# The state-space stage's output products one gate unit later, with one more buffer of four of its tiles

## The chip, the core and the metric

The kernel runs on one core of one Trainium2 chip. The metric is device microseconds of one execution; lower is better. Times of the trace are microseconds from the start of the profiled execution's span.

## What is computed

One layer of a flow-matching backbone on 128 context tokens and 1024 latent tokens, width 1024. The normed input `h` is multiplied by `w_in`, whose columns feed three things: the input of a bidirectional state-space branch (512 columns, 32 groups of 16), the input of a Fourier branch (512 columns), and two sigmoid gates of 1024 columns each. Cut to what matters here:

```
z = h @ p["w_in"]
u_s5, u_f, g_s5, g_f = ...        # 512, 512, 1024, 1024 columns
bu = einsum("nlgh,gph->nlgp", u, bb)              # into 64 complex states for each group
s = associative_scan(a, bu) + cumulated_a * h0    # along the tokens, in both directions
y = einsum("nlgp,ghp->nlgh", s_re, c_re) - einsum("nlgp,ghp->nlgh", s_im, c_im)
y = y + s5_d * u                                  # summed over both directions
m = sigmoid(g_s5) * (y_s5 @ w_proj_s5) + sigmoid(g_f) * (y_f @ w_proj_fft)
```

The layer goes on with `w_out`, a gated MLP and a last norm.

## The kernel before

Tokens are put in chunks of T = 8: 144 chunks (CC), of which 16 are context. The 32 groups are done in NB = 8 blocks of GQ = 4 groups, both directions side by side on the 128 partitions. A block q passes through three functions:

- `prep(q)` (`s5_prep` and `s5_prep2`) makes on DVE the tables W and G (lines 545 to 561), transposes G on PE (`gtr`, line 566), forms the in-chunk kernel on PE (`kx`, line 594) and DVE (KX, line 597), and sends KX by DRAM into the Toeplitz table T (lines 601 to 605). It begins by loading Bp and Cp, and by clearing `bb` (line 576), which the `kx` products of the block before must have read.
- `s5_run(q)` loads U, multiplies it on PE with G (the four PSUM tiles `v{q}_00`, `_02`, `_10`, `_12`, line 621), copies these into the states X on ACT (lines 625, 629) and DVE (lines 627, 630), and scans X in place on DVE: 14 steps of four dependent instructions (lines 636 to 639).
- `s5_out(q)` copies X, shifted, into Xo on ACT (lines 656 to 658) and multiplies on PE: T with U (line 666) and W with Xo (lines 667, 668), into the two PSUM tiles `y{q}_0`, `y{q}_2`.

The PSUM tiles `gtr`, `kx`, `v` and `y` take turns in three buffers (tag `aux`). So `v{q}_12` can begin only when DVE's copy of `v{q}_00` (line 630) has freed a buffer.

Between these calls stand nine gate units `gate(p)` of the order ORD = (0, 1, 2, 3, 4, 5, 8, 6, 7). Each has two halves f, and each half is 72 matmuls of 128x384 (lines 271 to 273; `g60_2` is the unit 6, half 0, token tile 2), in three precision-split products: the weights are split into a high part on ACT (line 93) and a low part on DVE (line 94, `wh_g600` and `wh_g601` for the two 512-column pieces of `g60`). The gates need nothing of the scans; they are PE work that can stand between the state-space steps. The unit after the loop is `uf20` (the second half of the Fourier input).

The order on each engine is not that of the code. A scheduler reorders the calls' instructions at build time, engine by engine, by its own estimates; each engine then runs its list strictly in that order, and waits at an instruction whose operands or buffers are not ready. SP's list holds the loads in the same way.

Of the kernel before, what the change touches and what calls it, by code (L numbers as in the profile page):

```python
# [10 lines left out]
F32 = mybir.dt.float32  # L11
# [18 lines left out]
T = 8  # L30
CP, CS = NP // T, NS // T
CC = CP + CS
GQ = 4
GU = 8
NB = G // GQ
# [2 lines left out]
NBG = 10  # L38
NUF = 3
NSG = 4  # L40
NW = 3
ORD = (0, 1, 2, 3, 4, 5, 8, 6, 7)
EPS = 1e-6
TW = 2 * 7 * 4 * 64
# [17 lines left out]
def tile_flow_step(ctx: ExitStack, tc: tile.TileContext, a, o):  # L62
# [459 lines left out]
    q5 = open_pool("q5", side="right")  # L522

    def s5_prep(q):
# [16 lines left out]

        W = q5.tile([128, 2, GQ * 128], F32, tag="W", bufs=NW, name=f"W{q}")
        Gt = q5.tile([128, 2, GQ * 128], F32, tag="G", bufs=NG, name=f"G{q}")
# [27 lines left out]
    def s5_prep2(q, gs, Bp, Cp, W, Win):  # L571
        bb = q5.tile([128, 3, 2, GQ * H + H], F32, tag="bb", name=f"bb{q}")
        b4 = bb[:, :, :, 0:GQ * H].rearrange("p v r (g h) -> p v r g h", g=GQ)
        bt1 = q5.tile([128, 240], F32, tag="KX", name=f"bt1{q}")[:, 0:2 * GQ * H].rearrange("p (r g h) -> p r g h", r=2, g=GQ)
        shb = [128, GQ, H]
        V.memset(bb, 0.0)
        for ri in range(2):
            fb = [fr2[:, r, gs].unsqueeze(2).to_broadcast(shb) for r in range(2)]
            V.tensor_tensor(b4[:, 0, ri], Bp[:, ri], fb[0], ALU.mult)
            V.tensor_tensor(bt1[:, ri], Bp[:, 1 - ri], fb[1], ALU.mult)  # L580
            V.tensor_tensor(b4[:, 0, ri], b4[:, 0, ri], bt1[:, ri],
                            ALU.subtract if ri == 0 else ALU.add)
        V.tensor_copy(bb[0:64, 1], bb[0:64, 0])
        V.tensor_copy(bb[64:128, 2], bb[64:128, 0])
        KX = q5.tile([128, GQ // 4, 240], F32, tag="KX", name=f"KX{q}")
        for aa in range(GQ // 4):
            ps = aux_tile(f"kx{q}_{aa}")
            for v, cs_ in ((2, slice(0, 112)), (0, slice(112, 128)), (1, slice(128, 240))):
                for ri in range(2):
                    for g4 in range(4):  # L590
                        g = 4 * aa + g4
                        src = (Cp[:, ri, g], W[:, ri, 128 * g:128 * g + 112],
                               W[:, ri, 128 * g + 16:128 * g + 128])[v]
                        PE.matmul(ps[32 * g4:32 * g4 + 32, cs_], bb[:, v, ri, H * g:H * g + 32], src,
                                  start=(ri == 0), stop=(ri == 1), skip_group_check=True)
            S.copy(out=KX[:, aa], in_=ps[:, 0:240])
            V.scalar_tensor_tensor(KX[:, aa, 112:128], eyeq, dq[:, GQ // 4 * q + aa:GQ // 4 * q + aa + 1],
                                   ps[:, 112:128], ALU.mult, ALU.add)
        kd = Kd[q]
        for g4 in range(4):  # L600
            SY.dma_start(out=kd[:, g4::4, :], in_=KX[32 * g4:32 * g4 + 16])
        Tm = q5.tile([128, GQ, 128], F32, tag="T", bufs=2, name=f"T{q}")
        win = bass.AP(tensor=kd.tensor, offset=kd.offset,
                      ap=[[16, T], [GQ * 240, H], [240, GQ], [1, 128]])
        SY.dma_start(out=Tm, in_=win)
        return W, Win, Tm

    def s5_run(q, Win):
        gs = slice(GQ * q, GQ * q + GQ)
        U = q5.tile([128, GQ, CC], F32, tag="U", bufs=2, name=f"U{q}")  # L610
        u0 = GQ * q % GU
        SY.dma_start(out=U, in_=Ud[GQ * q // GU].rearrange("s h (g c) -> (s h) g c", g=GU)[:, u0:u0 + GQ, :])
        X = q5.tile([128, 2, GQ, CC + 1], F32, tag="X", bufs=2, name=f"X{q}")
        V.memset(X[:, :, :, 0:1], 0.0)
        n = 0
        for ri in range(2):
            for g0 in range(0, GQ, 2):
                ng = 2
                ps = aux_tile(f"v{q}_{ri}{g0}")
                for g in range(ng):  # L620
                    PE.matmul(ps[:, CC * g:CC * g + CC], Win[:, ri, 128 * (g0 + g):128 * (g0 + g) + 128],
                              U[:, g0 + g, :], start=True, stop=True)
                v = ps[:, 0:CC * ng].rearrange("p (g c) -> p g c", g=ng)
                xg = X[:, ri, g0:g0 + ng]
                S.copy(out=xg[0:64, :, 1:CC + 1], in_=v[0:64])
                if n % 2:
                    V.tensor_copy(xg[64:128, :, CP + 1:CC + 1], v[64:128, :, CC - 1:CP - 1:-1])
                else:
                    S.copy(out=xg[64:128, :, CP + 1:CC + 1], in_=v[64:128, :, CC - 1:CP - 1:-1])
                V.tensor_copy(xg[64:128, :, 1:CP + 1], v[64:128, :, CP - 1::-1])  # L630
                n += 1
        def step(lv, dst, src):
            m = dst.shape[3]
            shp = [128, 2, GQ, m]
            A, B = (q5.tile([128, 2, GQ, CC // 2], F32, tag=f"{z}{q % 2}", name=f"{z}{q}_{lv}_{m}")[:, :, :, 0:m] for z in ("ta", "tb"))
            V.tensor_tensor(A, src, Sc[:, 0, lv, gs].unsqueeze(1).unsqueeze(3).to_broadcast(shp), ALU.mult)  # L636
            V.tensor_tensor(B, src, Sg[:, :, lv, gs].unsqueeze(3).to_broadcast(shp), ALU.mult)
            V.tensor_tensor(dst, dst, A, ALU.add)
            V.tensor_tensor(dst, dst, B[:, ::-1], ALU.add)  # L639

        for lv in range(4):
            d = 1 << lv
            step(lv, X[:, :, :, 2 * d:CC + 1:2 * d], X[:, :, :, d:CC + 1 - d:2 * d])
        V.tensor_copy(fin[:, :, gs], X[:, :, :, CP])
        V.tensor_copy(X[:, :, :, CP], h0[:, :, gs])
        for lv in range(4, 7):
            d = 16 << (lv - 4)
            step(lv, X[:, :, :, CP + d:CC:16], X[:, :, :, CP:CC - d:16])
        for lv in (3, 2, 1, 0):
            d = 1 << lv  # L650
            step(lv, X[:, :, :, 3 * d:CC + 1:2 * d], X[:, :, :, 2 * d:CC + 1 - d:2 * d])
        return U, X

    def s5_out(q, W, Tm, U, X):
        Xo = q5.tile([128, 2, GQ, CC], F32, tag="Xo", name=f"Xo{q}")
        S.copy(out=Xo[0:64], in_=X[0:64, :, :, 0:CC])
        S.copy(out=Xo[64:128, :, :, 0:CP], in_=X[64:128, :, :, CP - 1::-1])
        S.copy(out=Xo[64:128, :, :, CP:CC], in_=X[64:128, :, :, CC - 1:CP - 1:-1])
        ys = q5.tile([128, GQ, CC], F32, tag="gty", name=f"ys{q}")
        for g0 in range(0, GQ, 2):  # L660
            ng = 2
            ps = aux_tile(f"y{q}_{g0}")
            for g in range(ng):
                gg = g0 + g
                pg = ps[:, CC * g:CC * g + CC]
                PE.matmul(pg, Tm[:, gg, :], U[:, gg, :], start=True, stop=False)
                PE.matmul(pg, W[:, 0, 128 * gg:128 * gg + 128], Xo[:, 0, gg, :], start=False, stop=False)
                PE.matmul(pg, W[:, 1, 128 * gg:128 * gg + 128], Xo[:, 1, gg, :], start=False, stop=True)
            S.copy(out=ys[:, g0:g0 + ng, :], in_=ps[:, 0:CC * ng].rearrange("p (g c) -> p g c", g=ng))
        u0 = GQ * q % GU  # L670
        SY.dma_start(out=Yd[GQ * q // GU].rearrange("s h (g c) -> (s h) g c", g=GU)[:, u0:u0 + GQ, :], in_=ys)
# [5 lines left out]
    def gate(p):  # L677
        fu, j0 = (AF.Sigmoid, 8 + 2 * p) if p < 8 else (AF.Identity, 2 * p - 12)
        dst = [dram.tile([128, TOK], F32, tag=f"ind{j0 + f}", name=f"ind{j0 + f}") for f in range(2)]
        (SG if p < 8 else UF).extend(dst)  # L680

        def piece(f, t):
            return q5.tile([128, CH], F32, tag="sg", bufs=NSG, name=f"in{j0 + f}_{t}")

        in_unit(j0, f"g{p}", piece, lambda f, t, t_: S.dma_start(out=dst[f][:, CH * t:CH * t + CH], in_=t_), fu)

    def prep(q):
        return s5_prep2(q, *s5_prep(q))

    pre, run_ = [prep(0)], []  # L690
    gate(ORD[0])
    pre.append(prep(1))
    run_.append(s5_run(0, pre[0][1]))
    for q in range(NB):
        if q < NB - 1:
            run_.append(s5_run(q + 1, pre[q + 1][1]))
        if q:
            gate(ORD[q])
        if q == NB - 1:
            for p in ORD[NB:]:  # L700
                gate(p)
        s5_out(q, pre[q][0], pre[q][2], *run_[q])
        if q < NB - 2:
            pre.append(prep(q + 2))
    SY.dma_start(out=o["fin"], in_=fin)
    q5.release()
    pS.release()
# [1085 lines left out]
```

## Time and profile before

| | |
|---|---|
| runs | 1525.45 us median of 3 (1521.07 to 1526.0) |
| profiled execution | 1526.67 us, of which span 1524.9 us |
| PE busy | 1461.9 us (96%) |
| DVE busy | 940.8 us (62%) |
| ACT busy | 569.7 us (37%) |
| mean granted TensorE clock | 0.981 |
| state-space stage with its gates | from about 100 to 394 us |

The span is the time from the first to the last instruction, the rest of the execution's time lies around it. PE is TensorE's matmul, PEld its weight load, DVE VectorE, ACT ScalarE, POOL GpSimd, SP the queue of loads. The start-to-start time of two matmuls says how fast they stream; the duration in a row is longer, since they overlap. A note such as `[0.66 <-DVE X L630]` gives the engine's idle time ahead of an instruction and what ended it.

### The profile page before, as it was taken

How to read it: one execution, taken by the hardware profiler on the slowest of the kernel's cores; microseconds unless marked ns; L12 is line 12 of the kernel's file. 1: busy time of each engine (PE TensorE's matmuls, PEld its weight loads, DVE VectorE, ACT ScalarE, POOL GpSimd, SP SyncE). 2: the span in 40 equal slices, each digit the busy share in tenths (PEclk: the TensorE clock that was granted, in tenths of full speed). 3: DMA queues.
4: the chain of work that ended last, by engine and by line, in shares of the span. 5: the costliest groups of instructions: out<-in, count | busy, mean ns of one | idle time of the engine just before them, and what ended most of it. 6: DMA issues, size and time to landing. Idle time of an engine off the chain costs nothing. (4 is left out here: it accounts for less than half of the span.)

```text
span 1524.9 us, 23965 instructions
## 1 busy us (share of the span) xinstructions
PE 1461.9 (96%) x8999; PEld 1311.0 (86%) x8999; DVE 940.8 (62%) x1825; ACT 569.7 (37%) x1116; POOL 663.7 (44%) x599
## 2 busy tenths in 40 slices
PE   6999999999999999998899999999999999999995
PEld 3799999999968779776679999999999998887884
DVE  4557989996255335369964345553345567667778
ACT  6433344253454121355543433333333444112323
POOL 4920000000022111354687877977777972322354
PEclk8999999999989999999899999999999999999998
DMA  8333233232515653355532345444445558657523
GB/s 315 117 126 94 79 115 103 78 119 82 191 56 172 215 166 114 138 193 180 173 129 70 122 182 209 156 169 172 168 182 209 185 196 307 215 219 296 189 69 125
DMA packets 101984, 243.84 MB, mean 160 GB/s; under 512 B 15710, under 2 KB 46047, under 8 KB 101868
## 3 DMA queue, kind: packets, MB, share of 16 engines
q1 hardware_dynamic: 85452, 200.22, 38.2%
q10 hardware_dynamic: 16416, 42.08, 7.2%
q8 instruction: 71, 1.16, 0.3%
q14 instruction: 45, 0.37, 0.1%
HBM read 172.51 MB, written 69.74 MB: 159 GB/s over the span
## 5 line engine op out<-in xcount | busy, mean ns | idle before, releaser
L94 POOL TENSOR_TENSOR wh_glu<-ws_glu,wh_glu 128x512 fp32r<-128x512 f32 x4 | 5.1, 1274 | 334.9 <-ACT wh_glu L93 334.8
L271 PE MATMUL g<-h,wh_g 128*128 128x384 f32 (+1 forms) x432 | 147.0, 340 | 0.0
L272 PE MATMUL g<-h,wh_g 128*128 128x384 f32 (+1 forms) x432 | 146.9, 340 | 0.0
L273 PE MATMUL g<-h,wh_g 128*128 128x384 f32 (+1 forms) x432 | 146.6, 339 | 0.0
L1308 DVE TENSOR_TENSOR stg<-ra,stg 128x512 fp32r<-128x512 f32 x63 | 69.8, 1118 | 79.3 <-ACT stg L1307 79.2
L1416 POOL TENSOR_TENSOR wd<-wd,wd 128x512 f32<-128x512 f32 x25 | 36.4, 1469 | 112.2 <-DMA wd<-in_w_d 38.6
L273 PEld LDWEIGHTS g<-h,wh_g 128*128 128x128 f32 x432 | 81.2, 188 | 0.5 <-issue 0.5
L272 PEld LDWEIGHTS g<-h,wh_g 128*128 128x128 f32 x432 | 81.4, 188 | 0.0
L271 PEld LDWEIGHTS g<-h,wh_g 128*128 128x128 f32 x432 | 81.2, 188 | 0.2 <-issue 0.2
L94 POOL TENSOR_TENSOR wh_pj<-ws_pj,wh_pj 128x512 fp32r<-128x512 f32 x16 | 22.1, 1380 | 103.9 <-ACT wh_pj L93 94.3
L1469 DVE TENSOR_TENSOR acc<-acc,U 128x1024 f32<-128x1024 f32 x34 | 41.4, 1219 | 25.1 <-PE U L1450 24.8
L1307 ACT CAST stg<-ra 128x512 fp32r<-128x512 f32 x63 | 38.3, 617 | 34.2 <-DVE ra L1296 27.0
L963 DVE TENSOR_TENSOR wh_out<-ws_out,wh_out 128x512 fp32r<-128x512 f32 x32 | 33.7, 1069 | 24.6 <-ACT wh_out L962 24.6
L1450 PE MATMUL q<-B,A 128*128 128x512 f32 x192 | 45.4, 393 | 0.2 <-DVE tq L1599 0.2
L963 POOL TENSOR_TENSOR wh_out<-ws_out,wh_out 128x512 fp32r<-128x512 f32 x16 | 21.9, 1373 | 50.5 <-ACT wh_out L962 47.6
L1296 DVE TENSOR_TENSOR ra<-ra 128x512 f32<-128x512 f32 x36 | 43.7, 1214 | 0.3
L1450 PEld LDWEIGHTS q<-B,A 128*128 128x128 f32 x192 | 35.9, 187 | 8.8 <-DVE tq L1599 0.6
L923 DVE TENSOR_TENSOR sgc<-sgc,p 128x384 f32<-128x384 f32 x24 | 13.3, 554 | 48.4 <-PE p L106 48.4
L977 PE MATMUL o<-wh_out,m 128*128 128x512 f32 x96 | 36.7, 410 | 4.5 <-ACT scr0b L1059 4.5
L486 ACT ACTIVATE in<-g,sh_g 128x384 f32<-128x384 f32 x36 | 20.9, 582 | 53.3 <-PE g L273 52.7
L639 DVE TENSOR_TENSOR X<-X,tb 128x56 f32<-128x56 f32 (+10 forms) x88 | 39.5, 455 | 1.0
L636 DVE TENSOR_TENSOR ta<-X,Sg 128x56 f32<-128x56 f32 (+10 forms) x88 | 39.3, 446 | 1.2
(1550 smaller groups left out, 4523.1 us busy)
## 6 DMA issues: line engine op xcount, KB each, us to landing
ad<-stg ACTq DMA_DIRECT2D x60, 512.0 KB, 2.7
A<-ad SPq DMA_DIRECT2D x60, 512.0 KB, 6.9
wa<-in_w_ada SPq DMA_DIRECT2D x48, 512.0 KB, 6.0
ws_out<-in_w_out SPq DMA_DIRECT2D x24, 512.0 KB, 4.1
wd<-in_w_d SPq DMA_DIRECT2D x22, 512.0 KB, 8.4
ind<-in ACTq DMA_DIRECT2D x54, 192.0 KB, 1.9
ws_g<-in_w_in SPq DMA_DIRECT2D x18, 512.0 KB, 3.5
sgc<-ind SPq DMA_DIRECT2D x48, 192.0 KB, 3.8
```

Of the source, the lines that this page charges most:

```text
L271: PE.matmul(ps, w[:, 0, wsl], hi, start=first, stop=False)
L272: PE.matmul(ps, w[:, 0, wsl], lo, start=False, stop=False)
L273: PE.matmul(ps, w[:, 1, wsl], hi, start=False, stop=last)
L636: V.tensor_tensor(A, src, Sc[:, 0, lv, gs].unsqueeze(1).unsqueeze(3).to_broadcast(shp), ALU.mult)
L639: V.tensor_tensor(dst, dst, B[:, ::-1], ALU.add)
L963: (eng or PL).tensor_tensor(w[:, 1, :], src, f32(w[:, 0, :]), ALU.subtract)
L977: PE.matmul(p, mc[t][0][:, k, ts_], w[n][:, 0], start=(k == 0), stop=False)
L1296: V.tensor_tensor(a_[out], a_[x], a_[y], op)
L1307: S.copy(out=st_[:, 0], in_=src)
L1308: V.tensor_tensor(st_[:, 1], src, f32(st_[:, 0]), ALU.subtract)
L1450: PE.matmul(ps, A[:, va], B[:, vb], start=(first and ti == 0 and i == 0), stop=(last and ti == n - 1 and i == 2), skip_group_check=True)
L1469: V.tensor_tensor(dst, dst, ps, ALU.add)
```

## The change

In the loop over the blocks, the output products of block q-1 are now called after gate unit q, where before those of block q were; those of the last block are called after the loop, and the two last gate units also move behind it. The tiles W, T, U and X get one buffer more each, since they live longer.

```
-NW = 3
+NW = 4
...
-        Tm = q5.tile([128, GQ, 128], F32, tag="T", bufs=2, name=f"T{q}")
+        Tm = q5.tile([128, GQ, 128], F32, tag="T", bufs=3, name=f"T{q}")
...
-        U = q5.tile([128, GQ, CC], F32, tag="U", bufs=2, name=f"U{q}")
+        U = q5.tile([128, GQ, CC], F32, tag="U", bufs=3, name=f"U{q}")
...
-        X = q5.tile([128, 2, GQ, CC + 1], F32, tag="X", bufs=2, name=f"X{q}")
+        X = q5.tile([128, 2, GQ, CC + 1], F32, tag="X", bufs=3, name=f"X{q}")
...
+    def out(q):
+        s5_out(q, pre[q][0], pre[q][2], *run_[q])
+
     for q in range(NB):
         if q < NB - 1:
             run_.append(s5_run(q + 1, pre[q + 1][1]))
         if q:
             gate(ORD[q])
-        if q == NB - 1:
-            for p in ORD[NB:]:
-                gate(p)
-        s5_out(q, pre[q][0], pre[q][2], *run_[q])
+            out(q - 1)
         if q < NB - 2:
             pre.append(prep(q + 2))
+    for p in ORD[NB:]:
+        gate(p)
+    out(NB - 1)
```

No instruction of the computation is added or taken away. From `uf20` on the lists of all engines are the same in both kernels. In the state-space stage the scheduler makes other lists of them. Three places:

PE, before, where the products W0·Xo0 of block 0 (line 667) come up, in the gate half `g21`:

```order
L272 MATMUL g21_1_2483<-h1_97,wh_g211_2421 128x384
L273 MATMUL g21_1_2483<-h1_97,wh_g211_2421 128x384
L271 MATMUL g21_1_2483<-h1_97,wh_g211_2421 128x384
L667 MATMUL y0_0_1736<-Xo0_1731,W0_1192 128x144
L668 MATMUL y0_0_1736<-Xo0_1731,W0_1192 128x144
```

PE, of the change, the same products, in the gate half `g30`:

```order
L272 MATMUL g30_0_2728<-h0_96,wh_g300_2691 128x384
L273 MATMUL g30_0_2728<-h0_96,wh_g300_2691 128x384
L271 MATMUL g30_0_2728<-h0_96,wh_g300_2691 128x384
L667 MATMUL y0_0_2104<-Xo0_2099,W0_1192 128x144
L668 MATMUL y0_0_2104<-Xo0_2099,W0_1192 128x144
```

So these products stand 30 gate matmuls further on.

PE, before, at the last two state products of the stage, those of block 7 (lines `v7_10`, `v7_12`), in `g60`:

```order
L273 MATMUL g81_1_4043<-h1_97,wh_g811_3981 128x384
L271 MATMUL g60_2_4104<-h2_977,wh_g600_4097 128x386
L621 MATMUL v7_10_3799<-U7_3783,G7_3709 128x144 x2
L272 MATMUL g60_2_4104<-h2_977,wh_g600_4097 128x386
L621 MATMUL v7_12_3805<-U7_3783,G7_3709 128x144 x2
L666 MATMUL y6_0_4076<-U6_3393,T6_3391 128x144
```

PE, of the change, the same products, in `g80`:

```order
L273 MATMUL g80_0_3898<-h0_96,wh_g800_3861 128x384
L621 MATMUL v7_10_3777<-U7_3761,G7_3687 128x144 x2
L271 MATMUL g80_0_3898<-h0_96,wh_g800_3861 128x384
L621 MATMUL v7_12_3783<-U7_3761,G7_3687 128x144 x2
L272 MATMUL g80_0_3898<-h0_96,wh_g800_3861 128x384
```

Of the stage's 1296 gate matmuls 1010 stood ahead of `v7_12` and 286 behind it; now 898 stand ahead and 398 behind. Behind it before were also the products of blocks 6 and 7, now those of blocks 5, 6 and 7.

DVE, before, at X7's first copy (line 630, out of `v7_00`):

```order
L597 SCALAR_TENSOR_TENSOR KX7_3749<-eyeq_785,dq_783,kx7_0_3750 128x16
L644 COPY fin_712<-X6_3395 128x2x4
L645 COPY X6_3395<-h0_713 128x8
L636 TENSOR_TENSOR ta6_4_7_3447<-X6_3395,Sg_753 128x8x7
L637 TENSOR_TENSOR tb6_4_7_3448<-X6_3395,Sg_753 128x8x7
L630 COPY X7_3785<-v7_00_3787 64x2x16
L638 TENSOR_TENSOR X6_3395<-X6_3395,ta6_4_7_3447 128x8x7
```

DVE, of the change, at the same copy:

```order
L597 SCALAR_TENSOR_TENSOR KX7_3727<-eyeq_785,dq_783,kx7_0_3728 128x16
L636 TENSOR_TENSOR ta6_4_7_3425<-X6_3373,Sg_753 128x8x7
L637 TENSOR_TENSOR tb6_4_7_3426<-X6_3373,Sg_753 128x8x7
L639 TENSOR_TENSOR X5_2983<-X5_2983,tb5_1_35_3066 128x8x35
L638 TENSOR_TENSOR X6_3373<-X6_3373,ta6_4_7_3425 128x8x7
L630 COPY X7_3763<-v7_00_3765 64x2x16
L627 COPY X7_3763<-v7_02_3771 64x2x128
L636 TENSOR_TENSOR ta5_0_71_3071<-X5_2983,Sg_753 128x8x71
```

Block 5's last scan step (`ta5_0_71` and the three after it) and the low parts `wh_g600`, `wh_g601` stood ahead of this copy and now stand behind it; one instruction of 128x8x7 (line 638) now stands ahead. All else that DVE does ahead of it is the same set, in another order, with the scans of two blocks interleaved: pairs of neighbours in which the second needs the first's result (638 then 639, or 639 then 636, of one block) were 37 from the stage's start to `wh_g611`, and are 11.

## Rows read from the trace of the kernel before

**Rows 1.** Busy time by engine in three stretches; last are granted clock, DMA share, GB/s.

```profile
core 0: us, PE busy (x) PEld busy (x) DVE busy (x) ACT busy (x) POOL busy (x), PEclk, DMA share, GB/s
143.30:335.32 192.02, 186.08 (x1388) 179.55 (x1387) 183.76 (x497) 76.76 (x165) 0.00 (x0) 1.00 0.30 96
335.32:393.84 58.52, 57.03 (x341) 56.35 (x340) 34.87 (x88) 20.12 (x42) 0.00 (x0) 1.00 0.28 92
425.00:435.00 10.00, 6.54 (x23) 4.64 (x23) 7.51 (x24) 4.42 (x14) 0.00 (x0) 0.59 0.44 140
```

**Rows 2.** What PE waited for between 85 and 400 us: total, times, longest.

```profile
PE y L667 <- ACT Xo L658: 5.7, 4, 1.8
PE v L621 <- DVE X L630: 0.7, 1, 0.7
```

**Rows 3.** Timeline of PE: start, duration, instruction, and idle time ahead of it.

```profile
322.78 0.76 PE L621 MATMUL v<-U,G 128*128 128x144 f32 x4 [0.66 <-DVE X L630]
...
335.57 0.76 PE L621 MATMUL v<-U,G 128*128 128x144 f32 x4
...
365.89 0.34 PE L271 MATMUL g<-h,wh_g 128*128 128x386 f32 x1
...
390.82 0.33 PE L273 MATMUL g<-h,wh_g 128*128 128x384 f32 x1
391.00 0.41 PE L666 MATMUL y<-U,T 128*128 128x144 f32 x2
...
393.84 0.43 PE L271 MATMUL uf<-h,wh_uf 128*128 128x386 f32 x1
```

**Rows 4.** Timeline of DVE, the same columns.

```profile
143.30 0.19 DVE L630 COPY X<-v 64x32 f32<-64x32 f32 x1
...
169.75 0.23 DVE L638 TENSOR_TENSOR X<-X,ta 128x32 f32<-128x32 f32 x1
169.89 0.23 DVE L636 TENSOR_TENSOR ta<-X,Sg 128x48 f32<-128x48 f32 x1
...
314.23 0.75 DVE L636 TENSOR_TENSOR ta<-X,Sg 128x568 f32<-128x568 f32 x1
314.89 0.74 DVE L637 TENSOR_TENSOR tb<-X,Sg 128x568 f32<-128x568 f32 x1
...
317.42 0.68 DVE L94 TENSOR_TENSOR wh_g<-ws_g,wh_g 128x512 fp32r<-128x512 f32 x1
318.02 0.74 DVE L639 TENSOR_TENSOR X<-X,tb 128x568 f32<-128x568 f32 x1
...
335.32 0.20 DVE L630 COPY X<-v 64x32 f32<-64x32 f32 x1
...
338.38 0.22 DVE L638 TENSOR_TENSOR X<-X,ta 128x32 f32<-128x32 f32 x1
338.63 0.21 DVE L639 TENSOR_TENSOR X<-X,tb 128x32 f32<-128x32 f32 x1
```

**Rows 5.** What DVE waited for between 143.3 and 335.4 us: total, times, longest.

```profile
DVE X L627 <- ACT X L625: 2.0, 1, 2.0
DVE gt L560 <- DMA Bp<-in_b_p: 1.8, 2, 1.1
DVE X L630 <- ACT X L629: 0.5, 1, 0.5
DVE W L545 <- PE y L668: 0.5, 1, 0.5
```

**Rows 6.** Timeline of DVE early in the stage, where it clears `bb`.

```profile
119.91 0.46 DVE L576 MEMSET bb<- 128x480 f32 x1 [1.18 <-PE kx L594]
...
135.95 0.46 DVE L576 MEMSET bb<- 128x480 f32 x1 [0.34 <-PE kx L594]
```

**Rows 7.** Timeline of SP's queue behind the stage's last product.

```profile
394.56 0.33 SPq L671 DMA_DIRECT2D yd<-ys  x1
...
395.45 0.86 SPq L717 DMA_DIRECT2D uf<-ind  x2
```

## The prediction

> **What bounds the kernel now.** I read busy time by stage first, then PE's waits in the stage, then the timelines of PE and DVE where the two engines meet. Over the whole span PE is the full engine, but the share that matters is that of the state-space stage. From 143.30 us (the first copy of a state product on DVE) to 335.32 us (X7's first copy) PE is busy for 186.08 of 192.02 us, and DVE for 183.76 [rows 1]. Two engines are nearly full, each with 6 to 8 us to spare. Behind 335.32 this changes: in the last 58.52 us DVE is busy for 34.87 only.
>
> PE's waits in the whole stage are small: 5.7 us in four places for the shifted states Xo that ACT copies, ahead of the W·Xo products of line 667, and 0.7 us once for a copy on DVE [rows 2]. That one wait is the more telling. At 322.78 a state product stood still until DVE's line 630 had emptied a PSUM buffer [rows 3]. So DVE is not merely nearly full; PE already touches it. The second such place is X7's copy: it begins on DVE at 335.32 [rows 4], and the state product that needs its buffer, `v7_12`, begins on PE at 335.57 [rows 3], 0.25 us later. What PE does after that, gate matmuls and output products, waits for little, and `uf20` begins at 393.84. SP then stores and reloads what the stage leaves [rows 7], so the rest of the kernel, whose lists are the same in both kernels, moves with that moment.
>
> **The change part by part.**
>
> *The Xo waits.* The output products come 30 gate matmuls later at the place shown. A gate matmul streams at (390.82 − 365.89)/143 = 0.1743 us (143 steps between two matmuls of the gates' last stretch) [rows 3], so y0's first W product gets 5.2 us more, and each Xo wait is 1.8 us at most [rows 2]. The 5.7 us can go. That is the gain, if nothing else binds.
>
> The Trainium skill ("Perfetto Trace Analysis", section "Identifying Performance Opportunities") says that a gap which repeats on the engine that should be saturated can mean that there is not enough SBUF or PSUM for the next tile, a matter of buffer count. By that page alone four more buffers and a later consumer would close the four gaps, and the time would fall by about 6 us; the trace has the repeating gaps, but it has a second full engine too.
>
> *PE's work moved from ahead of DVE's deadline to behind it.* This is the main term. PE runs its list strictly in order, so whatever stands behind `v7_12` begins only after X7's first copy on DVE. Before, 286 gate matmuls and the products of two blocks stood there; now 398 gate matmuls and the products of three. One block's output products take 393.84 − 391.00 = 2.84 us [rows 3]. The work behind `v7_12` is therefore:
> 0.49 (`v7_12` itself, an estimate: the 0.76 of its kind's rows less what overlaps the next instruction) + 398 × 0.1743 + 3 × 2.84 = 0.49 + 69.39 + 8.52 = 78.4 us,
> where before it was 0.49 + 49.86 + 5.68 = 56.0. This sum for the kernel before, with 335.57 and 1.35 us for the waits left there, gives 393.0 against the row's 393.84, so it counts up to 0.9 us too little.
>
> The state products come earlier in PE's list by 112 gate matmuls, 19.5 us, and so ask for DVE's copy 19.5 us earlier; that is harmless only if DVE can be there earlier too. For an unchanged end, X7's copy would have to begin at 393.84 − 78.4 − 0.25 = 315.2 us.
>
> *When DVE gets there.* DVE's list ahead of that copy is nearly the same set. Moved behind it: four instructions of 128x568 at 0.66 us (314.23 to 314.89) and two low parts of weights (line 94) at 0.60 (317.42 to 318.02); moved ahead: one of 128x8x7 at 0.19, an estimate between the neighbours' 0.14 and 0.25 [rows 4]. Net 2.64 + 1.20 − 0.19 = 3.65 us less.
>
> The interleaved scans save something. A step that needs the one before it starts 0.25 us after it (338.38 to 338.63), an independent one 0.14 (169.75 to 169.89) [rows 4]; 26 dependent neighbours fewer are worth 26 × 0.11 = 2.8 us.
>
> The beginning costs something. DVE clears `bb` at 119.91 after 1.18 us of waiting for the `kx` products on PE, and at 135.95 after 0.34 us [rows 6]. These products now stand 10 and 9 gate matmuls later; PE is not late there, so DVE is, by about 9 × 0.1743 = 1.6 us.
>
> DVE's idle time in the stretch is 192.02 − 183.76 = 8.26 us, of which the named waits make 2.0 + 1.8 + 0.5 + 0.5 = 4.8 [rows 5]. If PE waits for DVE instead of DVE for others, most of these go. I take them all away, and leave the rest, which is the small change between instructions.
>
> X7's first copy: 335.32 − 3.65 − 2.8 + 1.6 − 4.8 = 325.7 us. That is 10.5 us after the 315.2 it would need.
>
> *Bounds of this term.* With no idle time at all, the dependent pairs out, and no late beginning, it is 143.30 + 183.76 − 3.65 − 26 × 0.08 (the busy part of such a pair: a pair's 0.22 against 0.14) = 321.3, 6.1 us late. With idle and pairs as before and the late beginning, 333.3, 18.1 us late. I take 10.5: DVE can't be fuller than full, and waits of DVE for other engines shrink when it is the late one.
>
> *Where PE's waits stand.* They don't come in one piece at `v7_12`. State products, `gtr` and `kx` share three PSUM buffers with the output products, and each block asks DVE earlier than before, so PE should wait at the products of blocks 3 to 7 in pieces of one to three us. The end is set by the last.
>
> *The gates' low parts on DVE* lie 18 to 24 us of DVE work later in the middle of the stage. Their lead over the gate matmuls that read them was 10 to 20 us; since PE is late too, I cost this at nothing. If the cover is gone, PE waits at a gate for line 94 instead, while DVE's end is the same.
>
> *Extra buffers* in themselves add no instruction. Xo is still copied by ACT, which is busy for 76.76 of 192 us [rows 1]; it hides that.
>
> *Sum.* `uf20` begins at 325.7 + 0.25 + 78.4 = 404.35, 10.5 us later than at 393.84. The profiled execution of before took 1526.67 us, 1.2 more than the median of the runs, 1525.45; against the median the change gives 1536.0.
>
> **The rivals.**
>
> *A: DVE doesn't bind, the Xo waits go.* Then the end comes about 6 us earlier: 1519.5. For this X7's copy must begin at 315.2 − 6 = 309 us, that is 166 us after 143.30, for work whose busy time is 183.76 − 3.65 − 2.1 = 178 us. [...] 0.05.
>
> *B: the two effects nearly cancel.* The end moves by less than 4.6 us (0.3%, about what a measurement of this kernel can tell from no change). X7's copy would have to begin by 319.8, 1.5 us under my lower bound; it needs, for instance, DVE starting before 143.30 by two us because the tables of blocks 0 and 1 come sooner. Time about 1528. 0.08.
>
> *C: more waits on top.* Two mechanisms. ACT's list is also in order, and it now has the copy of an old block's Xo between the two copies of a new X; if ACT is held there, DVE and PE are both. And PE's pieces of waiting may lower its clock: in the stage the granted clock is 1.00 (2.4 GHz), but in 425 to 435 us, where PE is busy for 6.54 of 10 us, it is 0.59, close to the 1.2 GHz level [rows 1]. A gate matmul at that level would take up to twice 0.1743; forty of them would add 7 us. The end would be 18 to 25 us later, about 1546. Against it: 10 us of waiting spread over 130 us leaves PE busy above 90%. 0.09.
>
> The Trainium skill ("TensorE: Matmul & The Clock Gate", section "HAM oscillation — how this bites in real kernels") describes C's second half: gaps in which PE idles bring the clock down, and the work behind them runs cold. The rows of 425 to 435 agree; that gaps of one to three us in a stretch otherwise full do it, no row of before shows.
>
> **How the numbers follow.** The main case, DVE late by 6 to 18 us, has 0.78, with 1536.0 as its likeliest and 1531.5 to 1543.5 as its bounds. A has 0.05, B 0.08, C 0.09. The range must leave out no more than 2 in 10: I take 1529.5 to 1543.5, which holds the main case, a little of B and of C. Faster (below 1520.9): A, 0.05. Same (1520.9 to 1530.0): B and the low rim of the main case, 0.09. Slower: 0.86.
>
> **What the profile of the changed kernel would show.** `uf20` begins on PE at about 404 (402 to 412). `v7_12` begins at about 326, 0.2 to 0.3 us after X7's first copy on DVE. The waits for Xo are gone or under 1 us; in their place PE's waits for DVE (lines 630, 597, 561 and 627) hold over 10 us between 200 and 326 us. DVE is idle for less than 4 us from its first state copy to X7's. The stretch from `uf20` to the end is as long as before. I am wrong if DVE still has its 8 us of idle time with PE on time (then its work was not what bound), if DVE's own start-to-start times shrink, or if PE's longest waits name ACT or a transfer.

## The result, and the profile after

The changed kernel takes 1535.22 us (median of 6 runs, 1529.73 to 1536.39), the kernel before 1525.72 (6 runs, 1520.29 to 1526.64). The ratio is 1.0069, 95% interval [1.0049, 1.0089]: slower by 9.5 us between the medians and by some 10.5 us by the ratio, where 1536.0 was forecast.

The two profiled executions differ by less, 1529.73 against 1526.67, and one must see where. From the first gate matmul to `uf20` (called the stage below) the kernel before takes 393.84 − 99.55 = 294.29 us and the changed one 403.00 − 97.37 = 305.63: 11.3 us more. Behind `uf20`, where the lists are the same, it is 1131.06 against 1124.90. So in this execution the changed kernel got back elsewhere, on equal lists, half of what it lost. One such place shows in equal stretches 301.6 us behind `uf20`; the eighth column (ahead of DMA share and GB/s) is the granted clock. Before:

```profile
695.44:770.84 75.40, 70.73 (x336) 52.63 (x334) 69.53 (x133) 41.41 (x68) 45.20 (x27) 0.90 0.54 183
```

Of the change, first the same stretch, then the stage from DVE's first state copy to X7's, and two pieces of it:

```profile
704.60:780.00 75.40, 70.25 (x352) 52.61 (x351) 70.09 (x139) 41.91 (x67) 43.12 (x26) 0.95 0.55 188
137.87:321.45 183.58, 169.08 (x1258) 161.34 (x1257) 180.20 (x505) 70.19 (x152) 0.00 (x0) 0.98 0.28 91
317.70:319.55 1.85, 1.85 (x8) 1.85 (x9) 1.85 (x8) 0.54 (x2) 0.00 (x0) 0.51 0.04 10
319.55:321.25 1.70, 1.70 (x7) 1.70 (x7) 1.67 (x6) 0.62 (x2) 0.00 (x0) 0.53 0.01 2
```

The higher clock is worth about (0.95 − 0.90) × 75.4 = 3.8 of the 6.2 us behind `uf20`, an estimate. Stages are therefore compared from the first gate matmul to `uf20`, and times by medians.

In the second row DVE is busy for 180.20 of 183.58 us (98%), PE for 169.08; before, in [rows 1], PE was idle for 5.9 us and DVE for 8.3. What PE waits for in the stage of the changed kernel (total, times, longest), against [rows 2]:

```profile
PE v L621 <- DMA U<-ud: 6.7, 4, 2.8
PE y L667 <- ACT Xo L658: 2.6, 2, 1.9
PE v L621 <- DVE KX L597: 2.1, 3, 1.1
PE gtr L566 <- DVE G L561: 1.5, 3, 0.7
PE y L666 <- DVE X L630: 0.7, 2, 0.4
PE gtr L566 <- DVE G L554: 0.6, 1, 0.6
PE v L621 <- DVE X L630: 0.2, 1, 0.2
```

The sum is 14.4 us, 7.3 before (three more of 0.4 us and less stand beside those of [rows 2]). The Xo waits shrank from 5.7 to 2.6; what came instead is the loads of U first, then DVE. The timeline shows how the last and longest of them comes about (all engines; SPq is SyncE's queue):

```profile
302.02 11.18 SPq L99 DMA_DIRECT2D ws_g<-in_w_in  x2
...
312.13 0.69 DVE L94 TENSOR_TENSOR wh_g<-ws_g,wh_g 128x512 fp32r<-128x512 f32 x1
...
313.30 0.37 SPq L612 DMA_DIRECT2D U<-ud  x1
...
317.70 2.22 PE L621 MATMUL v<-U,G 128*128 128x144 f32 x8 [2.77 <-DMA U<-ud]
...
321.45 0.20 DVE L630 COPY X<-v 64x32 f32<-64x32 f32 x1
...
324.39 0.65 PE L621 MATMUL v<-U,G 128*128 128x144 f32 x4
...
403.00 0.43 PE L271 MATMUL uf<-h,wh_uf 128*128 128x386 f32 x1
```

SyncE holds two weight loads from 302.02 on. The second, `ws_g61`, needs the buffer that DVE's low part `wh_g811` reads; that instruction runs only at 312.13. U7 is next in the queue, is issued at 313.30, and `v7_00` starts at 317.70. X7's first copy is on DVE at 321.45 and `v7_12` on PE at 324.39. So in this execution `v7_12` did not wait for that copy: from 319.55 to 324.39 PE works without a gap through the gate matmuls that its list has there. The last thing that PE waited for is U7.

The whole stage, first before, then of the change:

```profile
99.55:393.84 294.29, 286.86 (x2065) 278.14 (x2065) 248.24 (x663) 113.34 (x241) 0.00 (x0) 1.00 0.32 101
97.37:403.00 305.63, 291.13 (x2065) 281.90 (x2065) 244.67 (x664) 113.94 (x241) 0.00 (x0) 0.99 0.30 97
```

PE does the same 2065 instructions. Of the 11.3 us, 7.1 are its idle time, and 4.3 are a longer busy time.

### The profile page after: what moved, and what is told of

Same layout as the page of the kernel before. It is cut to its first block, busy times and chain, and to the rows that moved or that the text cites. A ratio compares the mean times of both kernels' runs of the same rounds, so it can differ in the third digit from the quotient of the medians.

```text
span 1527.9 us, 23962 instructions
## 1 busy us (share of the span) xinstructions
PE 1458.2 (95%) x8999; PEld 1310.1 (86%) x8999; DVE 937.8 (61%) x1825; ACT 571.1 (37%) x1116; POOL 660.3 (43%) x599
## 5 line engine op out<-in xcount | busy, mean ns | idle before, releaser
L637 DVE TENSOR_TENSOR tb<-X,Sg 128x56 f32<-128x56 f32 (+10 forms) x88 | 39.3, 448 | 0.0
L638 DVE TENSOR_TENSOR X<-X,ta 128x56 f32<-128x56 f32 (+10 forms) x88 | 39.1, 460 | 0.3
```

## The experiments

Behind `v7_12` each order leaves PE a fixed amount of work, counted as in the prediction (0.49 + 0.1743 for each gate matmul + 2.84 for each block's products). The sum is the measured start of `v7_12` plus this work. The last column is DVE's idle time from its first state copy to X7's first copy. Counted from the first gate matmul, in us:

| kernel | X7's first copy | v7_12 | work behind | sum | stage measured | PE waits | DVE idle |
|---|---|---|---|---|---|---|---|
| before | 235.8 | 236.0 | 56.0 | 292.0 | 294.3 | 7.3 | 8.7 |
| changed | 224.1 | 227.0 | 78.4 | 305.4 | 305.6 | 14.4 | 3.4 |
| e1, U on GpSimd's queue | 226.5 | 226.8 | 76.6 | 303.4 | 303.7 | 13.2 | 3.8 |
| e2, low parts on GpSimd | 243.1 | 243.9 | 78.4 | 322.3 | 324.4 | 28.0 | 3.5 |
| e3, the same in before | 247.5 | 247.7 | 67.5 | 315.2 | 319.7 | 24.3 | 14.0 |
| e4, buffers alone | 237.4 | 237.7 | 61.8 | 299.5 | 301.1 | 11.2 | 4.4 |
| e5, states later | 239.8 | 242.9 | 55.2 | 298.1 | 298.3 | 9.3 | 3.2 |
| e6, states later, U on GpSimd's queue | 242.0 | 245.2 | 55.2 | 300.4 | 300.7 | 10.0 | 5.3 |
| e7, states last | 246.9 | 247.2 | 53.1 | 300.2 | 300.4 | 11.8 | 7.4 |
| e8, before, Xo in halves | 240.0 | 240.3 | 56.2 | 296.5 | 297.9 | 8.1 | 11.5 |
| e9, U buffer alone | 235.1 | 235.6 | 60.9 | 296.5 | 297.3 | 10.4 | 4.6 |
| e10, W buffer alone | 248.6 | 249.0 | 45.6 | 294.5 | 295.6 | 9.0 | 17.3 |
| e11, W buffer, copies on ACT | 246.2 | 249.4 | 49.9 | 299.4 | 299.5 | 9.6 | 22.3 |
| e12, low parts on ACT | 224.0 | 224.3 | 78.0 | 302.3 | 302.6 | 14.6 | 3.8 |

Three things are to be read here. The sum meets the stage within 0.1 to 2.3 us (4.5 in e3, whose last Xo wait of 2.47 us lies behind `v7_12`): behind `v7_12` PE waits for 1.4 us at most elsewhere. Since it starts from the measured `v7_12`, it says nothing of what sets that date. In ten of fourteen kernels `v7_12` begins within 0.8 us of X7's first copy, in seven of them 0.25 us behind it. In the other four (the changed kernel, e5, e6, e11) it begins 2.9 to 3.2 us behind the copy, and PE's last wait lies earlier: for U at `v7_00` in the changed kernel and in e11, for DVE's line 630 at 314.27 in e5 and at 310.19 in e6. And DVE is nearly without idle time in the changed kernel, e1, e2, e4, e5, e9 and e12 (3.2 to 4.6 us), but not in the kernel before, e3, e8, e10 and e11 (8.7 to 22.3).

**e1, the loads of U off SyncE's queue.**

```
-        SY.dma_start(out=U, in_=Ud[...]...)
+        PL.dma_start(out=U, in_=Ud[...]...)
```

> The changed kernel with the eight loads of U issued from GpSimd's queue instead of SyncE's; nothing else is edited (the last state product v7_12 then has 908 gate matmuls ahead and 388 behind, 898 and 398 in the changed kernel). Theory DVE: VectorE is the limit (busy 180.2 of 183.6 us up to X7's first copy at 321.45), and PE's waits for U only show its lateness by another route. Then the waits for U are replaced by waits for DVE (lines 630, 597, 561), X7's first copy stays at 319 to 322, and the stage from the first gate matmul to uf20 shrinks from 305.6 to no less than 300 to 303 us; the time stays 0.2 to 0.6% above the kernel before. Theory queue: U stuck on SyncE's queue behind weight loads is the limit by itself. Then the 6.7 us of waits for U and the cold matmuls behind the longest (about 1.5 us) go without replacement: stage 297 us, time within 0.2% of the kernel before.

1533.13 us against 1522.46, ratio 1.0078 [1.0061, 1.0094]; stage 303.72. PE's waits in the stage:

```profile
PE v L621 <- DVE KX L597: 7.2, 4, 2.2
PE y L667 <- ACT Xo L658: 2.5, 2, 1.8
PE gtr L566 <- DVE G L561: 1.2, 3, 0.6
```

and X7's first copy with the product that needs its buffer:

```profile
325.57 0.20 DVE L630 COPY X<-v 64x32 f32<-64x32 f32 x1
...
325.82 0.76 PE L621 MATMUL v<-U,G 128*128 128x144 f32 x4
```

The 6.7 us of waits for U are gone, and 7.2 us of waits for DVE's line 597 stand in their place (2.1 in the changed kernel). `v7_12` is 0.25 us behind X7's copy, as the prediction had it. The expectation had X7's copy at 319 to 322; it came at 325.57, 2.4 us later after the first gate matmul than in the changed kernel, and the stage is 0.7 us over its 300 to 303. So the queue was a second route of the same lateness, and taking it away gave back 1.9 us of stage and nothing that the times show.

**e2 and e3, the gates' low parts on GpSimd**, in the changed kernel and in the kernel before.

```
-            w = weight(a["w_in"][j0 + f], f"{nm}{f}", eng=V)
+            w = weight(a["w_in"][j0 + f], f"{nm}{f}", eng=PL if nm[0] == "g" else V)
```

> The changed kernel with the low parts of the gates' weights (line 94, 36 instructions of 0.60 us on VectorE) made by GpSimd, which does nothing in this stage. Theory DVE: VectorE has some 19 us less ahead of X7's first copy, which moves from 321 to 303 to 306 us; PE is on time and its waits fall under 4 us in all; stage about 288 to 291 us (294.3 in the kernel before, 305.6 in the changed one), time about 0.3 to 0.5% under the kernel before. Theory queue: the weight buffers are freed by GpSimd as soon as ScalarE has made the high part, so U's loads come earlier too; the same sign. Theory clock or ScalarE (waits for ScalarE's copies and a lowered clock are the price): the stage stays over 297 us, and PE waits for Xo or for ScalarE's X copies.

> The kernel before with the same edit, low parts of the gates' weights on GpSimd. Theory DVE: the four waits for Xo (5.7 us) are VectorE's lateness as well, since ScalarE copies Xo when the scan has ended; they go, the stage falls to 288 to 291 us as in the run with the change, and the change adds nothing. If the waits for Xo are a matter of order (products too close behind the scan), they stay at 4 to 6 us, the stage stays at 292 to 295 us, and the changed order with the same relief is 4 to 6 us faster than this.

Both missed by far: 1552.32 us, ratio 1.0201 [1.0182, 1.0219], stage 324.4; and 1544.97, ratio 1.0153 [1.0132, 1.0175], stage 319.7, with 15.3 us of waits for Xo. None of the theories as put held: in e2 the stage stays over 297 us as the last of them says, but of the 28.0 us of PE's waits 15.0 are for DVE's line 597 and 6.2 for Xo. The timeline of e2, DVE and POOL, shows why:

```profile
199.00 1.27 POOL L94 TENSOR_TENSOR wh_g<-ws_g,wh_g 128x512 fp32r<-128x512 f32 x1 [15.46 <-ACT wh_g L93]
...
199.17 1.71 DVE L639 TENSOR_TENSOR X<-X,tb 128x576 f32<-128x576 f32 x1
200.80 0.74 DVE L636 TENSOR_TENSOR ta<-X,Sg 128x568 f32<-128x568 f32 x1
...
204.30 6.41 POOL L94 TENSOR_TENSOR wh_g<-ws_g,wh_g 128x512 fp32r<-128x512 f32 x1 [4.03 <-ACT wh_g L93]
...
209.58 1.23 DVE L584 COPY bb<-bb 64x160 f32<-64x160 f32 x1
```

While GpSimd makes one low part in 1.27 us, DVE's instruction, 0.75 us else ([rows 4]: 0.75 for 128x568), takes 1.71. The next low part takes 6.41 us, while DVE's two-input instructions follow each other; it ends about when a copy of DVE (L584) is held up in its turn, 1.23 us (its line's mean is 0.24 in the kernel before and 0.63 here). These are the far ends: of e2's 36 low parts most take about 1.3 us. Moving 0.60 us off DVE costs it up to 1 us. The two kernels are thus a test with a slower DVE instead of a lighter one: both stages grow, by 18.8 and 25.4 us, and X7's copy in both comes later.

**e4, the buffers alone**: NW = 4 and T, U, X with three buffers, the loop as before.

> The kernel before with the one more buffer of W, T, U and X, its loop left as it was. In its order 319 gate matmuls and the products of two blocks stand behind v7_12, so X7's first copy would be wanted by 331.8 us for an unchanged end, 335.3 in the kernel before. Theory DVE: the copy comes at 330 to 334, the stage is 292 to 297 us long, the time within 0.2% of before. Theory queue: no wait for U, since a third buffer lets its load go early; waits for Xo as before, 5 to 6 us; the time as before. If the buffers and not the moved products do the harm, the stage is over 300 us.

1532.12 us, ratio 1.0062 [1.0045, 1.0079]; stage 301.1, over the 300 that was named as the mark of harm by the buffers. X7's copy came at 237.4, not at the 230.5 to 234.5 expected (330 to 334 us in the times of the kernel before); with 61.8 us behind it the sum gives 299.5. Most of the loss is there without the moved output products: 6.8 of the 11.3 us of the stage, and by the runs' times nearly all of it (1.0062 against 1.0069, with intervals that overlap). What the buffers changed is the order: `v4_12` has 607 gate matmuls ahead (735 before), `v6_12` 872 (978). PE asks DVE earlier, and its longest group of waits is one for DVE:

```profile
PE v L621 <- DVE KX L597: 6.1, 4, 2.3
PE v L621 <- DVE X L630: 1.7, 2, 1.5
PE y L667 <- ACT Xo L658: 1.2, 1, 1.2
```

**e5, e6, e7, the state products called later**, all with the change's buffers and its moved output products. In e5:

```
     for q in range(NB):
-        if q < NB - 1:
-            run_.append(s5_run(q + 1, pre[q + 1][1]))
         if q:
             gate(ORD[q])
+        if q < NB - 1:
+            run_.append(s5_run(q + 1, pre[q + 1][1]))
+        if q:
             out(q - 1)
```

> The changed kernel with one call moved: the state products and scan of block q+1 (s5_run) are called after gate unit q instead of before it. Buffers and output products stay as the change has them. v7_12 then has 1031 gate matmuls ahead and 265 behind (898 and 398 in the changed kernel, 1010 and 286 before). Theory DVE: VectorE can be at X7's first copy 224 to 227 us after the first gate matmul, as in the changed kernel and with U on GpSimd's queue; work behind v7_12 is 0.49 + 265 x 0.1743 + 3 x 2.84 = 55.2 us, so the copy is wanted only by 239 for the stage of before. PE waits under 4 us in all, the stage is 287 to 291 us (294.3 before, 305.6 changed), the time 0.2 to 0.5% under the kernel before. Theory harm of the buffers or of the moved output products in themselves: the stage stays over 297 us, since both are still there.

> The same with the loads of U issued from GpSimd's queue. Theory DVE: if the run with the later state products still waits for U, those waits go and nothing replaces them, since VectorE is ahead of PE there; stage 287 to 289 us. If it does not wait for U, both are equal within 1 us.

e6 is e5 with the loads of U as in e1; in e7 the call stands behind `out(q - 1)`.

> The changed kernel with s5_run(q+1) called after gate unit q and after the output products of q-1. v7_12 has 1027 gate matmuls ahead, 269 behind, and the products of blocks 6 and 7. Theory DVE: work behind v7_12 53.1 us, X7's copy wanted only by 241 us after the first gate matmul; PE waits under 5 us, stage 287 to 291 us. If the place of the output products ahead of the state products costs (PSUM buffers held while they wait for Xo), waits for Xo of over 4 us appear and the stage is 292 to 296 us.

e5: 1528.20 us, ratio 1.0023 [1.0010, 1.0036], stage 298.3. e6: 1528.13, ratio 1.0033 [1.0019, 1.0047], stage 300.7. e7: 1530.99, ratio 1.0044 [1.0028, 1.0060], stage 300.4. With nothing but the place of the state products, about two thirds of the loss of the changed kernel are gone, though buffers and late output products are still there. But the stage missed the 287 to 291 us, in e5 by 7, and in all three runs it is over the 297 us that the expectation of e5 set as the mark of a harm of the buffers or the moved products in themselves. So that rival is not excluded for the last third. I had taken over X7's copy from the changed kernel (224 to 227); it came at 239.8, since the new order put more of DVE's other work ahead of it: all 44 instructions of block 6's scan (lines 636 to 639; the code makes 11 steps of four, and the 14 steps named with `s5_run` are a miscount), 19 in the changed kernel. PE's waits in e5:

```profile
PE v L621 <- DVE X L630: 3.0, 2, 2.5
PE v L621 <- DMA U<-ud: 2.4, 1, 2.4
PE y L667 <- ACT Xo L658: 1.8, 1, 1.8
PE gtr L566 <- DVE X L630: 1.5, 1, 1.5
```

In e6 the wait for U is replaced too: the waits for line 630 at the state products rise from 3.0 to 6.1 us. My "nothing replaces them" was wrong there, in the direction of the DVE theory. In e7 no wait is for Xo, and 11.2 of PE's 11.8 us are for line 630; neither branch of its expectation held.

**e8, the kernel before with Xo copied in halves** of two groups, six copies for three.

> The kernel before with Xo copied in two halves of two groups each (six copies instead of three), so that the first output products of a block wait for half of it only. Theory DVE: the waits for Xo fall from 5.7 to 2 to 3 us, but v7_12 still begins 0.25 us behind X7's first copy, 235 to 236 us after the first gate matmul, and the stage shrinks by no more than 2 us. Theory order alone (the waits for Xo are what the stage loses): the stage shrinks by 3 to 4 us, time 0.2 to 0.25% less.

1528.73 us, ratio 1.0030 [1.0014, 1.0047]; stage 297.9, 3.6 us longer, against both expectations. The waits for Xo fell to 3.9 us, and 3.5 us for U appeared; X7's copy came at 240.0. Even a part cure of the Xo waits gave nothing; the order changed with it, so this does not price the waits alone.

**e9, e10, e11, single buffers in the kernel before**: U alone; W alone; W alone with all state copies of line 627 on ScalarE.

> The kernel before with one more buffer of U and nothing else. The order then brings the state products forward as with all four buffers: v2_12 has 442 gate matmuls ahead (483 before), v4_12 662 (735), v6_12 889 (978), v7_12 982 (1010); behind v7_12 stand 314 and the products of two blocks, 60.9 us. Theory DVE: VectorE is as late as ever, X7's first copy 235 to 237 us after the first gate matmul, so the stage is 296 to 299 us (294.3 before), with more waits of PE for VectorE; time 0.2 to 0.5% over before. Theory queue: U arrives early, so there is nothing to wait for and the stage is no longer than before.

> The kernel before with one more buffer of W and nothing else. The order then moves the state products back: v2_12 has 527 gate matmuls ahead (483 before), v4_12 769 (735), v6_12 1009 (978), v7_12 1070 (1010); behind v7_12 stand 226 and the products of two blocks, 45.5 us. Theory DVE: PE asks 6 to 10 us later than before, its waits fall to 2 to 4 us, X7's first copy comes 236 to 244 us after the first gate matmul, the stage is 287 to 291 us, the time 0.2 to 0.45% under before. If VectorE gets as much more to do ahead of each copy as PE asks later, the stage is 293 to 295 us and the time the same.

> The same with all state copies of line 627 made by ScalarE, 16 instructions of 0.43 us less on VectorE; v7_12 has 1045 gate matmuls ahead, 251 behind, 49.9 us of work. Theory DVE: VectorE has 6 us less up to X7's first copy, which comes at 230 to 238 us after the first gate matmul; stage 287 to 290 us, time 0.25 to 0.5% under before. If ScalarE's list is the limit (Xo stands behind more copies), waits for Xo exceed 6 us and the stage is 292 us or more.

e9: 1527.42 us, ratio 1.0016 [1.0003, 1.0029], stage 297.3, X7's copy at 235.1, as the DVE theory had them; the time is just under its 0.2 to 0.5%, and of the waits 7.2 us are for Xo. e10: 1526.54, ratio 1.0015 [1.0000, 1.0030], stage 295.6. e11: 1528.71, ratio 1.0022 [1.0008, 1.0036], stage 299.5. In e10 PE asks up to 10 us later, and DVE is later by as much: X7's copy at 248.6, with 35 instructions of block 6's scan ahead (18 before). That is near the second branch of its expectation. e11 missed: DVE had 6 us less of copies, but X7's copy was at 246.2, and PE waited 4.9 us for Xo.

In these two a full DVE is not what made the copy late: it was idle for 17.3 and 22.3 us ahead of it. In e10 DVE is busy for 192.35 of 209.67 us up to X7's copy (first row), and its longest group of waits (second row) is at the clearing of a new X, which has two buffers there, for ACT's copies of an old one:

```profile
137.54:347.21 209.67, 200.96 (x1478) 194.82 (x1477) 192.35 (x530) 82.33 (x176) 0.00 (x0) 1.00 0.30 95
DVE X L614 <- ACT Xo L658: 5.3, 2, 2.8
```

**e12, the low parts off DVE without GpSimd** (ScalarE copies the weights instead of a subtraction).

```
-        (eng or PL).tensor_tensor(w[:, 1], src, f32(w[:, 0]), ALU.subtract)
+        S.copy(out=w[:, 1], in_=src)
```

> The changed kernel with the gates' low parts off VectorE in another way than in the run on GpSimd: line 94 becomes a copy of the weights on ScalarE (0.6 us each, 36 of them). This leaves out the subtraction, so the low products are not the remainders; shapes and counts of all products are unchanged. PE's list is nearly that of the run on GpSimd (v5_12 has 656 gate matmuls ahead, there 649, in the changed kernel 716; v7_12 900, there 898). Theory DVE: VectorE has 19 us less ahead of X7's first copy, which comes at 203 to 212 us after the first gate matmul (224 in the changed kernel); the order asks for X5 11 us earlier than before, which eats most of the relief at block 5: PE waits 8 to 10 us in all, stage 295 to 300 us (305.6 in the changed kernel). If what made the run on GpSimd long (324.4) is its order or its lighter VectorE, this one is over 310 us too; if it is that VectorE's instructions run longer beside GpSimd's, they have their old lengths here (0.75 us for 128x568).

1531.87 us, ratio 1.0066 [1.0046, 1.0087], stage 302.6. DVE's 128x568 instructions have their 0.75 us again, and the stage is 21.8 us shorter than in e2, with almost the same PE list. From DVE's first state copy to X7's, e2 (first row) and e12 (second row) have about as many DVE instructions and as little idle time, but in e2 they take 20.3 us more:

```profile
136.84:341.54 204.70, 176.53 (x1285) 169.06 (x1284) 201.23 (x514) 74.78 (x159) 37.63 (x20) 0.95 0.27 83
138.82:323.52 184.70, 170.03 (x1283) 163.75 (x1282) 180.92 (x513) 84.59 (x179) 0.00 (x0) 0.99 0.29 91
```

PE's waits for U in e2 are 1.2 us, and none of its waits is at a gate for a low part. So GpSimd's work beside DVE was what made e2 long, and these two runs show most directly that in such an order DVE's time sets the end: DVE longer by 20.3 us, X7's copy later by 19.0, the stage longer by 21.8. But X7's copy of e12 did not come at 203 to 212; the timeline has it where it was (lines are three higher in this file):

```profile
323.52 0.20 DVE L633 COPY X<-v 64x32 f32<-64x32 f32 x1
...
323.77 0.39 PE L624 MATMUL v<-U,G 128*128 128x144 f32 x1
```

323.52 − 99.51 = 224.0 after the first gate matmul, 224.1 in the changed kernel. The 28 low parts that left (16.8 us) made room for 29 more scan instructions ahead of that copy: 44 of each of blocks 5 and 6, against 40 and 19. DVE was as full as in the changed kernel (idle for 3.8 us).

None of the variants beats the kernel before; the nearest are e9 and e10, with ratios of 1.0016 and 1.0015 whose intervals begin at 1.0003 and 1.0000.

## Why the prediction was right, and where it was not

**The mechanism and the sum.** Counted from the first gate matmul, the prediction has X7's copy at 226.1, `v7_12` at 226.4 and `uf20` at 304.8; measured are 224.1, 227.0 and 305.6. That the end is met within 1 us is in part luck: the copy came 2.0 us too early for the sum, and `v7_12` stood 2.7 us further behind it than forecast. e1, where it stands 0.25 us behind the copy, ends at 303.7. The work behind `v7_12` was given as 78.4 us and is 403.00 − 324.39 = 78.6. DVE's idle time in the stretch was to be under 4 us; it is 3.38. The late beginning, 1.6 us, shows in the two `bb` clears, 1.75 and 1.54 us later after the first gate matmul than in [rows 6].

**The step that failed** is the one on the gates' low parts, costed "at nothing". They did come too late for something: not for the matmuls that read them, but for the weight buffers. SyncE's queue stood behind them, and U7 behind SyncE. That is why PE's waits name U with 6.7 us and DVE with 5.1, where "over 10" was written for DVE, and why `v7_12` is 2.9 us behind X7's copy instead of 0.25. One of the prediction's own signs of being wrong came true with it, that PE's longest waits name a transfer. e1 shows that this was a detour: without it about the same time is spent waiting for DVE, and 1.9 us of the stage are saved.

**The Xo waits** were to be "gone or under 1 us"; 2.6 are left. The gain of 5.7 us on which rival A rests was 3.1, and bought nothing. By the Trainium skill ("Perfetto Trace Analysis", section "Identifying Performance Opportunities") more buffers could close such repeating gaps. Here they closed half, and others opened.

**Rival C, the clock,** was there in part. After the wait of 2.77 us the granted clock was 0.51 and 0.53, close to the lower of its two levels, for 3.55 us, about 1.7 us lost, and about as much after the wait of 1.94 us that ends at 196.89 (granted clock 0.84 from 194 to 205 us). Together that is an estimate of 3.4 of the 4.3 us by which PE's busy time grew; the prediction gave the clock no term in the main case. DVE's date can cover the earlier loss, but not the later one: `v7_12` came 2.94 us behind X7's copy with no wait between, so that loss went into the end. e1, without it, has a stage 1.9 us shorter.

**Behind `uf20`** the stretch was to be as long as before; in the profiled execution it was 6.2 us shorter, on equal lists, so the changed kernel's profiled time says less of the change than its median does.

**A slip of name:** 143.30 us, called the first state copy on DVE, is the sixth; the first is at 138.47. The sum uses 143.30 only as the start of a stretch and is not touched.

**Wider than predicted.** The prediction spoke of the moved products. e4 shows that buffers alone cost 6.8 us of the 11.3, e5 that about two thirds of the loss hang on the place of the state products. The lists are made at build time; with the buffers of e4 and e9 they let PE ask earlier (with that of W alone, in e10, later), and where DVE is relieved, as in e12, they fill it with other work. That the estimates behind them take DVE for faster than it is, is the natural reading; no run shows these estimates, so it stays argued. The moved output products without the buffers were not tried.

## What to carry to other kernels

When two engines are nearly full, find the last instruction at which one waits for the other, and count the work that the order leaves behind it: date plus work is the end, and here it met thirteen of fourteen kernels within 2.3 us. Look whether the wait is really there: in four of them the last wait came earlier. More buffers change the order too; no run with more of them was faster here, and where the engine that must empty them was nearly full (e4, e9), PE waited more. A wait's label names the last link; take that link away, as in e1, before taking it for the cause.

## What the runs showed of the hardware that was not expected

GpSimd and VectorE held each other up when both ran instructions with two SBUF inputs. A 128x576 addition took 1.71 us on DVE beside GpSimd's subtraction of 128x512, and a GpSimd subtraction of 1.27 us took 6.41 while DVE was busy. The Trainium skill ("GPSIMD Engine Reference", section "1. Specifications") lists this contention, with DVE instructions that have two SBUF inputs; the runs agree for the two-input ones. It also names DVE instructions in a two-port mode; a DVE copy with one input was held up here too (1.23 us, mean 0.24 without GpSimd), but no run shows in which mode it was.

The granted clock did not fall after every such wait of PE. In the changed kernel it fell to 0.50, the 1.2 GHz level, after waits of 1.94 us (first row; the wait ends at 196.89) and 2.77 us, but not after the 2.12 us at 284.55 (second row). In e10 it stayed at 1.00 behind a wait of 2.83 us that ends at 324.87 (third row).

```profile
198.30:201.60 3.30, 3.30 (x15) 3.30 (x14) 3.30 (x9) 1.28 (x4) 0.00 (x0) 0.50 0.36 124
284.55:289.00 4.45, 4.45 (x28) 4.38 (x28) 4.41 (x18) 1.64 (x4) 0.00 (x0) 1.00 0.10 36
324.87:340.00 15.13, 15.13 (x101) 15.06 (x102) 14.69 (x30) 8.52 (x18) 0.00 (x0) 1.00 0.18 66
```
